# RWKV-7 scan: rows of beta and kappa swapped for the last four heads, right-hand sides laid out by chunk parity

## Chip, core and metric

The kernel runs on one core of a Trainium2 chip. The metric is device time in microseconds (us) of one execution; lower is better. Three timed runs of the kernel before are at hand, and one further execution was recorded by the hardware profiler.

Engine names as the profile has them: PE is the matrix engine and PEld its weight loads, DVE the vector engine, ACT the scalar engine, POOL the general one, SP the queue that issues nearly all DMAs. A name such as L592 is line 592 of the kernel before, unless the text says that it is a line of the changed kernel.

## What is computed

Two decoder layers on 512 tokens of width 1024. In each layer a gated FFN, then three token mixers beside each other on one normalised input (RWKV-7, latent attention, HGRN2), then a second FFN. The change lies in RWKV-7 alone, whose core is this recurrence over the tokens, for 8 heads of width 64:

```
def step(state, inp):
    r_t, w_t, k_t, v_t, kk_t, a_t = inp
    sa = jnp.einsum('bhvk,bhk->bhv', state, -kk_t)
    state = (state * w_t[:, :, None, :]
             + sa[..., None] * (kk_t * a_t)[:, :, None, :]
             + v_t[..., None] * k_t[:, :, None, :])
    return state, jnp.einsum('bhvk,bhk->bhv', state, r_t)
```

## The kernel before

**Chunks.** The recurrence is done in 8 chunks of 64 tokens (`CH`, `NC`). A head pair p (0 to 3) holds heads 2p and 2p+1; e picks the head in the pair; four tiles t of 128 tokens hold two chunks each, and u is the chunk's parity. Partitions 0 to 63 and 64 to 127 are the halves `U[0]` and `U[1]`.

**Before the scan.** `prep_keys` writes, for each pair, `BK`: beside each other in the columns of a tile beta and kappa (keys times the rate `a`, and keys), so that the matmul L483 of `rwkv_invert` puts beta products of a chunk of parity u in rows `U[u]` of the matrix `GM`, and kappa products in rows `U[1-u]`. L486 masks them on DVE. `prep_v` transposes the values; since kappa rows sit in the half that is not the chunk's own, ACT first copies the values with the two chunks of a tile exchanged (L453, two copies per pair). L489 (ACT) gathers the 32x32 diagonal blocks. L492 to L507, 31 steps of two DVE operations between transposes, invert them. L524 and L527 (PE, 32x32 tiles) join the blocks to `tt`, the inverse of each chunk.

**The scan** (`rwkv_scan`). First L567 forms the part of each right-hand side that comes from the values, and L568 copies it to `gv`. Then, for each chunk c of parity u:

- L575 (ACT) copies the values into the kappa half of `zv`;
- L583 (PE) multiplies the state by alpha, 8 matmuls, all into rows `U[u]`, one bank of PSUM for each e;
- L586 (DVE) adds `gv`: four additions on 64 partitions;
- L592 (PE) multiplies by the inverse: 8 matmuls, all reading and writing the half `U[u]`;
- L593 (ACT) negates the result into the other half of `zv`;
- L599 (PE) forms the new state's increment, L603/L605 and L607 (DVE) the new state;
- L611 and L615 (PE) form the output and L617 (ACT) stores it.

Each step needs the one above it. An fp32 matmul of this part is one row of the instruction order and two records of the trace (8 rows of L583, x16 in the trace).

**Fill.** So that PE has something to do meanwhile, projections of the other two mixers and of the gates are mixed in. One unit is 24 matmuls of 128x512 (L251 to L253), here called fills. `pump` releases units at named places by the table `PUMP`; a scheduler in the framework then decides at build time, by its own model of times, between which instructions of PE's queue the fills go, and the order on every other engine. The engines follow that order strictly. The weights of a unit are split into two parts, one by ACT (L208) and one by DVE (L209).

Of the kernel before, what the change touches and what calls it, by code (L numbers as in the profile page):

```python
# [14 lines left out]
AF = mybir.ActivationFunctionType  # L15
ALU = mybir.AluOpType
# [4 lines left out]
P = 128  # L21
# [3 lines left out]
NT = T // P  # L25
# [4 lines left out]
CH = 64  # L30
# [276 lines left out]
class Rwkv:  # L307
# [88 lines left out]
    def prep_keys(self, p, l):  # L396


        nc = self.nc
        S = self.S  # L400
        k, sw, a, kk = S["k"], S["sw"], S["a"], S["kk"]
        ch = lambda x: x.rearrange("p (c x) -> p c x", x=CH)
        tu = lambda x: x.rearrange("p (t u x) -> p t u x", u=2, x=CH)
        nc.vector.scalar_tensor_tensor(kk[:, p, :], k[:, p, :], S["k_k"](p), kk[:, p, :], op0=ALU.mult, op1=ALU.mult)
        al, d = S["AR"][p // 2][:, p % 2, 0], S["AR"][p // 2][:, p % 2, 1]
        bk = S["BK"][p // 2][:, p % 2]
        di = self.t2()
        nc.scalar.activation(d, sw[:, p, :], AF.Exp, scale=-DECAY)
        nc.scalar.activation(di, sw[:, p, :], AF.Exp, scale=DECAY)

        nc.vector.tensor_mul(ch(al)[:, :, 1:], ch(kk[:, p])[:, :, 1:], ch(d)[:, :, :CH - 1])
        nc.scalar.copy(ch(al)[:, :, 0:1], ch(kk[:, p])[:, :, 0:1])
        nc.vector.tensor_mul(kk[:, p], kk[:, p], a[:, p])
        nc.vector.tensor_mul(bk[:, :, 0::3, :], tu(kk[:, p]), tu(di))

        nc.scalar.activation(a[:, p, :], a[:, p, :], AF.Identity, scale=self.vec("rwkv_k_a", l, p), bias=self.oka[:, 4 * l + p:4 * l + p + 1])
        nc.vector.tensor_mul(k[:, p, :], k[:, p, :], a[:, p, :])
        nc.vector.tensor_mul(bk[:, :, 1:3, :], tu(k[:, p]), tu(di))
        nc.gpsimd.tensor_copy(self.DL[:, p], ch(d)[:, :, CH - 1])

    def prep_r(self, p, l):
# [7 lines left out]
    def prep_v(self, p, l):  # L429


        nc = self.nc
        S = self.S
        r, v, vres = S["r"], S["v"], S["vres"]
        if p == 0:
            S["vn"] = self.slot(10, (P, NT, T))
            if vres is not None:
                S["vup"] = self.t2()
                nc.sync.dma_start(out=S["vup"][32:64, :], in_=self.a["rwkv_vres_up"][0])
        if vres is not None:  # L440
            ps = self.psum("a")
            nc.tensor.matmul(ps, S["vup"][32:64, p * P:(p + 1) * P], vres[32:64, :], start=True, stop=True)
            sg, vf = self.t2(), self.t2()
            nc.sync.dma_start(out=vf, in_=self.v_first[:, p, :])
            nc.scalar.activation(sg, ps, AF.Sigmoid, bias=self.vec("rwkv_v0", 0, p))
            nc.vector.tensor_sub(vf, vf, v[:, p, :])
            nc.vector.tensor_mul(sg, sg, vf)
            nc.vector.tensor_add(v[:, p, :], v[:, p, :], sg)
        elif l == 0:
            nc.sync.dma_start(out=self.v_first[:, p, :], in_=v[:, p, :])  # L450
        vs = self.t2(shape=(P, NT, 2, CH))
        for u in range(2):
            nc.scalar.copy(vs[:, :, 1 - u, :], v[:, p].rearrange("p (t u x) -> p t u x", u=2, x=CH)[:, :, u, :])  # L453
        ps = self.psum("a", (P, NT, 2, CH))
        for t in range(NT):
            self.transpose(ps[:, t].rearrange("p e x -> p (e x)"), vs[:, t].rearrange("p u x -> p (u x)"))
        mean = self.tile([P, 2 * NT], "mean", bufs=2)
        nc.vector.tensor_reduce(mean, ps.rearrange("p t e x -> p (t e) x"), axis=AX.X, op=ALU.add)
        nc.vector.scalar_tensor_tensor(S["vn"][:, :, p * P:(p + 1) * P].rearrange("p t (e x) -> p t e x", x=CH),
                                       mean.rearrange("p (t e) -> p t e", e=2).unsqueeze(3).broadcast_to([P, NT, 2, CH]), -1.0 / CH,  # L460
                                       ps, op0=ALU.mult, op1=ALU.add)
        ps = self.sums(self.ones64, r[:, p, :])
        nc.vector.tensor_mul(v[:, p, :], v[:, p, :], ps)

    def rwkv_invert(self):


        nc = self.nc
        S = self.S
        GM = S["GM"] = [self.slot(i, (P, 2, NC, P)) for i in (0, 1, 6, 7)]  # L470
        ad = self.m4((P, 4, 2, NT, 32))
        mask = self.c("tri").unsqueeze(1).broadcast_to([P, 4, P])
        for p in range(4):
            self.pump("A4", p)

            for i in range(2):
                ps = [self.psum("a", (P, 4, P)) for _ in range(2)]
                for c in range(4):
                    cc = 4 * i + c
                    for e in range(2):  # L480
                        q = slice(64 * e, 64 * e + 64)
                        bk = S["BK"][p // 2][q, p % 2].rearrange("p t z x -> p (t z x)")
                        nc.tensor.matmul(ps[e][:, c, :], bk[:, P * cc:P * cc + P], S["AR"][p // 2][q, p % 2, :, cc * CH:(cc + 1) * CH],  # L483
                                         start=True, stop=True)
                for e in range(2):
                    nc.vector.tensor_mul(GM[p][:, e, 4 * i:4 * i + 4, :], ps[e], mask)  # L486
            for b in range(4):
                q = slice(32 * b, 32 * b + 32)
                nc.scalar.copy(ad[q, p], GM[p][q, :, b // 2::2, 32 * (b % 2):32 * (b % 2) + 32])  # L489
        nc.sync.dma_start(out=self.yd, in_=S["v"])  # L490
        ac = [self.m4((P, 32, 32)) for _ in range(2)]
        nc.vector.transpose(out=ac[0].rearrange("p s t -> p t s"), in_=ad.rearrange("p a e t x -> p x (a e t)"))  # L492
        a, tmp = ac
# [15 lines left out]
        for i in range(2):  # L509
# [8 lines left out]
            for half in range(2):  # L518
                for n in range(16):
                    h, t = 4 * i + n // 4, n % 4  # L520
                    for u in range(2):
                        up, dn = slice(64 * u, 64 * u + 32), slice(64 * u + 32, 64 * u + 64)
                        if half == 0:
                            nc.tensor.matmul(n21[dn, n, :], GM[h // 2][up, h % 2, 2 * t + u, 32:64], tu[up, 16 * i + n, :],  # L524
                                             start=True, stop=True, tile_position=(64 * u, 64 * u + 32))
                        else:
                            nc.tensor.matmul(n21[up, n, :], x[dn, n, :], tt[dn, n, dn], start=True, stop=True,  # L527
                                             tile_position=(64 * u + 32, 64 * u))
# [20 lines left out]
    def rwkv_scan(self, l):  # L549
# [6 lines left out]
        al = lambda p: S["AR"][p // 2][:, p % 2, 0]  # L556
        rho = lambda p: S["AR"][p // 2][:, p % 2, 1]
        bk = lambda p, c: S["BK"][p // 2][:, p % 2].rearrange("p t (u z) x -> p (t u) (z x)", u=2)[:, c]
        gv = [self.m4((P, 2, 2, NT, CH)) for _ in range(2)]
        for p in range(4):  # L560
            self.pump("A7", p)
            ps = self.psum("a", (P, 2, NT, CH))
            for e in range(2):
                h = 2 * p + e
                for t in range(NT):
                    for u in range(2):
                        nc.tensor.matmul(ps[U[u], e, t, :], GM[p][U[1 - u], e, 2 * t + u, 0:64], vn[U[1 - u], t, 64 * h:64 * h + 64], start=True, stop=True)  # L567
            nc.scalar.copy(gv[p // 2][:, p % 2], ps)  # L568
        for c in range(NC):
            self.pump("A8", c)  # L570
            t, u = c // 2, c % 2
            ck = slice(c * CH, (c + 1) * CH)

            zv = self.t2(shape=(P, 4, 2, CH))
            nc.scalar.copy(zv[U[1 - u]], vn[U[1 - u], t].rearrange("p (h e x) -> p h e x", e=2, x=CH))  # L575
            if c == 0:
                rhs = lambda p, e: gv[p // 2][U[0], p % 2, e, 0, :]
            else:
                r = self.t2(shape=(P, 4, 2, CH))
                ps = [self.psum("a", (P, 4, CH)) for _ in range(2)]  # L580
                for p in range(4):
                    for e in range(2):
                        nc.tensor.matmul(ps[e][U[u], p, :], al(p)[U[e], ck], st[U[e], 0, p, :], start=True, stop=True)  # L583
                for i in range(2):
                    for e in range(2):
                        nc.vector.tensor_add(r[U[u], 2 * i:2 * i + 2, e, :], ps[e][U[u], 2 * i:2 * i + 2, :], gv[i][U[u], :, e, t, :])  # L586
                rhs = lambda p, e: r[U[u], p, e, :]
            z = self.psum("z", (P, 4, 2, CH))
            for p in range(4):
                for e in range(2):  # L590
                    h = 2 * p + e
                    nc.tensor.matmul(z[U[u], p, e, :], S["tt"][h // 4][U[u], (h % 4) * 4 + t, U[u]], rhs(p, e), start=True, stop=True)  # L592
            nc.scalar.activation(zv[U[u]], z[U[u]], AF.Copy, scale=-1.0)  # L593
            y = self.psum("y", (P, 4, CH))
            if c < NC - 1:
                ns = self.psum("n", (P, 4, CH))
# [824 lines left out]
```

## Time and profile before

| | |
|---|---|
| three runs, median (lowest to highest) | 2718.49 us (2716.76 to 2718.83) |
| the profiled execution, its own time | 2718.67 us |
| its span, first to last instruction | 2716.9 us |
| mean granted PE clock | 0.995 |
| scan of the first layer, L567 to the last L615 | 597.40 to 653.6 us |
| scan of the second layer ends (last L617) | about 2005.8 us |

In a timeline row the first number is the start, the second the length, both in us; xN counts merged records, and what stands in square brackets is the idle time before them and what ended it. A matmul's length is longer than the distance to the next one, since matmuls are pipelined; so what PE pays is read from the distance between starts. In the table of stretches PEclk is the clock that was granted to PE as a share of the full one.

### The profile page before, as it was taken

How to read it: one execution, taken by the hardware profiler on the slowest of the kernel's cores; microseconds unless marked ns; L12 is line 12 of the kernel's file. 1: busy time of each engine (PE TensorE's matmuls, PEld its weight loads, DVE VectorE, ACT ScalarE, POOL GpSimd, SP SyncE). 2: the span in 40 equal slices, each digit the busy share in tenths (PEclk: the TensorE clock that was granted, in tenths of full speed). 3: DMA queues.
4: the chain of work that ended last, by engine and by line, in shares of the span. 5: the costliest groups of instructions: out<-in, count | busy, mean ns of one | idle time of the engine just before them, and what ended most of it. 6: DMA issues, size and time to landing. Idle time of an engine off the chain costs nothing. (4 is left out here: it accounts for less than half of the span.)

```text
span 2716.9 us, 42586 instructions
## 1 busy us (share of the span) xinstructions
PE 2668.8 (98%) x17669; PEld 2319.0 (85%) x17669; DVE 1771.6 (65%) x2507; ACT 1342.8 (49%) x2129; POOL 58.1 (2%) x121
## 2 busy tenths in 40 slices
PE   8999999999999999999999999999999999999999
PEld 7999888877787789998899998877777877899987
DVE  6776377743866767785468764477448676678843
ACT  4544346345657544444344443464455585444532
POOL 0000010000000010000000000000000000100000
PEclk9999999989999999999999999999999999999999
DMA  4333332334421542333313333233353315322332
GB/s 143 108 110 124 120 113 95 117 113 141 135 92 55 183 163 64 123 104 115 124 61 96 103 131 128 97 106 106 101 171 110 100 67 180 140 94 94 112 114 78
DMA packets 223519, 307.72 MB, mean 113 GB/s; under 512 B 11857, under 2 KB 181053, under 8 KB 221789
## 3 DMA queue, kind: packets, MB, share of 16 engines
q1 hardware_dynamic: 223324, 304.99, 34.1%
q8 instruction: 139, 2.28, 0.3%
q14 instruction: 56, 0.45, 0.1%
HBM read 269.84 MB, written 35.13 MB: 112 GB/s over the span
## 5 line engine op out<-in xcount | busy, mean ns | idle before, releaser
L251 PE MATMUL b<-xhi,wh 128*128 128x256 f32 (+1 forms) x2176 | 734.4, 337 | 0.0
L253 PE MATMUL b<-xhi,wl 128*128 128x256 f32 (+1 forms) x2176 | 733.7, 337 | 0.0
L252 PE MATMUL b<-xlo,wh 128*128 128x256 f32 (+1 forms) x2176 | 732.0, 336 | 0.0
L208 ACT CAST wh<-ws 128x1024 fp32r<-128x1024 f32 (+5 forms) x448 | 393.5, 889 | 654.4 <-PE b L252 285.6
L209 DVE TENSOR_TENSOR wl<-ws,wh 128x1024 fp32r<-128x1024 f32 (+5 forms) x448 | 453.4, 1022 | 271.0 <-ACT wh L208 263.0
L251 PEld LDWEIGHTS b<-xhi,wh 128*128 128x128 f32 x2176 | 414.7, 191 | 43.9 <-issue 3.7
L253 PEld LDWEIGHTS b<-xhi,wl 128*128 128x128 f32 x2176 | 414.7, 191 | 40.9 <-issue 1.6
L252 PEld LDWEIGHTS b<-xlo,wh 128*128 128x128 f32 x2176 | 414.8, 191 | 40.5 <-issue 1.7
L252 PE MATMUL b<-s,wh 128*128 128x256 f32 (+1 forms) x1120 | 344.7, 308 | 1.7 <-DVE s L209 1.7
L251 PE MATMUL b<-s,wh 128*128 128x256 f32 (+1 forms) x1120 | 344.2, 308 | 0.0
L253 PE MATMUL b<-s,wl 128*128 128x256 f32 (+1 forms) x1120 | 343.7, 307 | 0.0
L208 ACT CAST wh<-m 128x1024 fp32r<-128x1024 f32 x144 | 151.3, 1051 | 230.4 <-PE b L252 98.9
L251 PE MATMUL b<-wh,t 128*128 128x512 f32 x576 | 224.2, 389 | 0.0
L252 PE MATMUL b<-wl,t 128*128 128x512 f32 x576 | 224.1, 389 | 0.0
L253 PE MATMUL b<-wh,t 128*128 128x512 f32 x576 | 224.1, 389 | 0.0
L251 PEld LDWEIGHTS b<-s,wh 128*128 128x128 f32 x1120 | 213.9, 191 | 11.9 <-DVE s L1006 1.2
L252 PEld LDWEIGHTS b<-s,wh 128*128 128x128 f32 x1120 | 214.0, 191 | 11.8 <-DVE s L209 2.2
L253 PEld LDWEIGHTS b<-s,wl 128*128 128x128 f32 x1120 | 214.0, 191 | 10.3 <-DVE wl L209 0.5
L209 DVE TENSOR_TENSOR wl<-m,wh 128x1024 fp32r<-128x1024 f32 x144 | 174.0, 1224 | 32.5 <-ACT wh L208 32.5
L209 DVE TENSOR_TENSOR t<-s,t 128x512 fp32r<-128x512 f32 x80 | 55.0, 691 | 158.5 <-PE b L252 154.4
L251 PEld LDWEIGHTS b<-wh,t 128*128 128x128 f32 x576 | 108.1, 188 | 23.0 <-ACT t L1204 0.6
L253 PEld LDWEIGHTS b<-wh,t 128*128 128x128 f32 x576 | 108.1, 188 | 22.4
(324 smaller groups left out, 3965.4 us busy)
## 6 DMA issues: line engine op xcount, KB each, us to landing
ws<-in_w_in_dram SPq DMA_DIRECT2D x58, 1024.0 KB
ws<-in_ffn_w_up_dram SPq DMA_DIRECT2D x44, 1024.0 KB
ws<-in_ffn_w_down_dram SPq DMA_DIRECT2D x44, 1024.0 KB
ws<-in_ffn_w_gate_dram SPq DMA_DIRECT2D x43, 1024.0 KB
gd<-f SPq DMA_DIRECT2D x48, 256.0 KB
t<-gd SPq DMA_DIRECT2D x48, 256.0 KB
s<-cd SPq DMA_DIRECT2D x8, 1024.0 KB
ws<-in_w_o_dram SPq DMA_DIRECT2D x8, 1024.0 KB
```

What stands on the lines that cost most here:

```text
L208: self.nc.scalar.copy(hi, src)
L209: self.nc.vector.tensor_sub(lo, src, hi.bitcast(F32))
L251: nc.tensor.matmul(out, whi, xhi, start=start, stop=False, **kw)
L252: nc.tensor.matmul(out, whi, xlo, start=False, stop=False, **kw)
L253: nc.tensor.matmul(out, wlo, xhi, start=False, stop=stop, **kw)
```

## The change

For pairs 2 and 3 (the last four heads) beta and kappa change places in `BK`. Their rows in `GM` change halves with them: for these pairs the chunk's own products now lie in half `U[1-u]`. `prep_v` needs no exchanging copy for these pairs and transposes the values directly. `gv` is now indexed by parity (two buffers, one for each u) instead of by pair.

In the scan, `B = (U[u], U[1 - u])` gives the half of a pair: `B[0]` for pairs 0 and 1, `B[1]` for pairs 2 and 3. The right-hand sides of all eight heads so fill all 128 partitions, and two additions of 128x128 take the place of four of 64x128. The matmuls with alpha (L593 of the changed kernel) and with the inverse (L601 there) run in the order of pairs 0, 2, 1, 3, so that neighbours lie in different halves. The inverse's loop has e outside. The result is negated by two engines, ACT for `B[0]` (L602 there) and DVE for `B[1]` (L603 there), 64x256 each, and the values are copied into `zv` by two ACT copies of 64x256 (L585 there). The names of lines in the changed kernel: alpha L593, additions L595, inverse L601, increment L609, new state L613/L615, output L621 and L625.

```
-        nc.vector.tensor_mul(bk[:, :, 0::3, :], tu(kk[:, p]), tu(di))
+        sides = (bk[:, :, 0::3, :], bk[:, :, 1:3, :])
+        nc.vector.tensor_mul(sides[p // 2], tu(kk[:, p]), tu(di))
...
-        nc.vector.tensor_mul(bk[:, :, 1:3, :], tu(k[:, p]), tu(di))
+        nc.vector.tensor_mul(sides[1 - p // 2], tu(k[:, p]), tu(di))
...
-        vs = self.t2(shape=(P, NT, 2, CH))
-        for u in range(2):
-            nc.scalar.copy(vs[:, :, 1 - u, :], v[:, p].rearrange("p (t u x) -> p t u x", u=2, x=CH)[:, :, u, :])
+        vs = v[:, p]
+        if p < 2:
+            vs = self.t2()
+            for u in range(2):
+                nc.scalar.copy(vs.rearrange("p (t u x) -> p t u x", u=2, x=CH)[:, :, 1 - u, :], v[:, p].rearrange("p (t u x) -> p t u x", u=2, x=CH)[:, :, u, :])
...
-            nc.scalar.copy(zv[U[1 - u]], vn[U[1 - u], t].rearrange("p (h e x) -> p h e x", e=2, x=CH))
+            for i in range(2):
+                nc.scalar.copy(zv[B[1 - i], 2 * i:2 * i + 2], vn[B[1 - i], t].rearrange("p (h e x) -> p h e x", e=2, x=CH)[:, 2 * i:2 * i + 2])
...
-                r = self.t2(shape=(P, 4, 2, CH))
-                ps = [self.psum("a", (P, 4, CH)) for _ in range(2)]
-                for p in range(4):
+                r = self.t2(shape=(P, 2, 2, CH))
+                ps = [self.psum("a", (P, 2, CH)) for _ in range(2)]
+                for p in (0, 2, 1, 3):
                     for e in range(2):
-                        nc.tensor.matmul(ps[e][U[u], p, :], al(p)[U[e], ck], st[U[e], 0, p, :], start=True, stop=True)
-                for i in range(2):
-                    for e in range(2):
-                        nc.vector.tensor_add(r[U[u], 2 * i:2 * i + 2, e, :], ps[e][U[u], 2 * i:2 * i + 2, :], gv[i][U[u], :, e, t, :])
+                        nc.tensor.matmul(ps[e][B[p // 2], p % 2, :], al(p)[U[e], ck], st[U[e], 0, p, :], start=True, stop=True)
+                for e in range(2):
+                    nc.vector.tensor_add(r[:, e], ps[e], gv[u][:, :, e, t, :])
...
-            z = self.psum("z", (P, 4, 2, CH))
-            for p in range(4):
-                for e in range(2):
-                    h = 2 * p + e
-                    nc.tensor.matmul(z[U[u], p, e, :], S["tt"][h // 4][U[u], (h % 4) * 4 + t, U[u]], rhs(p, e), start=True, stop=True)
-            nc.scalar.activation(zv[U[u]], z[U[u]], AF.Copy, scale=-1.0)
+            z = self.psum("z", (P, 2, 2, CH))
+            for e in range(2):
+                for p in (0, 2, 1, 3):
+                    q = B[p // 2]
+                    nc.tensor.matmul(z[q, p % 2, e, :], S["tt"][p // 2][q, (2 * p + e) % 4 * 4 + t, q], rhs(p, e), start=True, stop=True)
+            nc.scalar.activation(zv[B[0], 0:2], z[B[0]], AF.Copy, scale=-1.0)
+            nc.vector.tensor_scalar(zv[B[1], 2:4], z[B[1]], -1.0, None, op0=ALU.mult)
```

The scheduler answers with another order. On PE, in a chunk of the first layer's scan, from the last fills after the alpha matmuls to the first increments, this stood there before (the third and the later L592 rows use the second `tt` buffer):

```order
L253 MATMUL b_801_5778<-xhi_92,wl_5775 128x512
L251 MATMUL b_801_5778<-xhi_92,wh_5774 128x512
L592 MATMUL b_787_5675<-t_5660,s_714_5075 64x64
L252 MATMUL b_801_5778<-xlo_93,wh_5774 128x512
L592 MATMUL b_787_5675<-t_5660,s_714_5075 64x64 x3
L592 MATMUL b_787_5675<-t_5660,s_715_5076 64x64 x4
L253 MATMUL b_801_5778<-xhi_92,wl_5775 128x512
L251 MATMUL b_801_5778<-xhi_92,wh_5774 128x512
L252 MATMUL b_801_5778<-xlo_93,wh_5774 128x512
L253 MATMUL b_801_5778<-xhi_92,wl_5775 128x512
L599 MATMUL b_789_5686<-t_5658,s_574_4140 64x64 x4
```

The same place on PE in the changed kernel, where L601 is the multiplication by the inverse:

```order
L253 MATMUL b_799_5774<-xhi_92,wl_5771 128x512
L601 MATMUL b_777_5612<-t_5599,s_712_5069 64x64
L601 MATMUL b_777_5612<-t_5599,s_713_5070 64x64
L601 MATMUL b_777_5612<-t_5599,s_712_5069 64x64
L601 MATMUL b_777_5612<-t_5599,s_713_5070 64x64
L601 MATMUL b_777_5612<-t_5599,s_712_5069 64x64
L601 MATMUL b_777_5612<-t_5599,s_713_5070 64x64
L601 MATMUL b_777_5612<-t_5599,s_712_5069 64x64
L601 MATMUL b_777_5612<-t_5599,s_713_5070 64x64
L251 MATMUL b_799_5774<-xhi_92,wh_5770 128x512
L252 MATMUL b_799_5774<-xlo_93,wh_5770 128x512
L253 MATMUL b_799_5774<-xhi_92,wl_5771 128x512
```

The eight inverse matmuls stand in one piece and alternate between the two buffers (and halves), where fills cut them in two or three pieces before. Counted from the first L567 to the last output matmul of one layer, the order of before has 88 fills in 29 pieces, that of after 83 fills in 20 pieces; the five others follow behind the scan. Both layers have the same counts.

In the second layer, on ACT, the end of the block gathering stood so before (L453 the exchanging copies of the last pair, L489 the gathering, `wh<-ws` a split of fill weights):

```order
L453 COPY t_17020<-s_2317_16176 128x4x64 x2
L208 CAST t_17032<-s_2315_16174 128x512
L489 COPY m_17043<-s_2464_17039 32x256 x4
L489 COPY m_17043<-s_2465_17040 32x256 x4
L489 COPY m_17043<-s_2466_17041 32x256 x4
L208 CAST wh_17297<-ws_17253 128x1024
L489 COPY m_17043<-s_2467_17042 32x256 x4
```

The same place in the changed kernel, where the gathering is L493:

```order
L208 CAST t_17022<-s_2313_16170 128x512
L493 COPY m_17033<-s_2460_17029 32x256 x4
L493 COPY m_17033<-s_2461_17030 32x256 x4
L493 COPY m_17033<-s_2462_17031 32x256 x4
L493 COPY m_17033<-s_2463_17032 32x256 x4
L208 CAST wh_17287<-ws_17243 128x1024
```

The copies are gone there, and the weight split stands behind the last gathering, no longer ahead of it. On PE the second layer has 9 fills fewer ahead of L524, which now come between L527 and the transposes of `BK` that follow it. On DVE one mask (L486) now stands ahead of the last pair's value statistics, and the weight split that stood ahead of L492 stands behind it. In the first layer the order ahead of the scan is the same on PE; there, and from some way behind the scan on, only single operations changed places.

More of the change, by code (lines that the diff above doesn't have):

```diff
@@ L450, in prep_v @@
             nc.sync.dma_start(out=self.v_first[:, p, :], in_=v[:, p, :])
-        vs = self.t2(shape=(P, NT, 2, CH))
-        for u in range(2):
-            nc.scalar.copy(vs[:, :, 1 - u, :], v[:, p].rearrange("p (t u x) -> p t u x", u=2, x=CH)[:, :, u, :])
+        vs = v[:, p]
[3 more added lines that the diff above has]
+                nc.scalar.copy(vs.rearrange("p (t u x) -> p t u x", u=2, x=CH)[:, :, 1 - u, :], v[:, p].rearrange("p (t u x) -> p t u x", u=2, x=CH)[:, :, u, :])
         ps = self.psum("a", (P, NT, 2, CH))
         for t in range(NT):
-            self.transpose(ps[:, t].rearrange("p e x -> p (e x)"), vs[:, t].rearrange("p u x -> p (u x)"))
+            self.transpose(ps[:, t].rearrange("p e x -> p (e x)"), vs[:, t * P:(t + 1) * P])
         mean = self.tile([P, 2 * NT], "mean", bufs=2)
@@ L488, in rwkv_invert @@
                 q = slice(32 * b, 32 * b + 32)
-                nc.scalar.copy(ad[q, p], GM[p][q, :, b // 2::2, 32 * (b % 2):32 * (b % 2) + 32])
+                nc.scalar.copy(ad[q, p], GM[p][q, :, (b // 2 + p // 2) % 2::2, 32 * (b % 2):32 * (b % 2) + 32])
         nc.sync.dma_start(out=self.yd, in_=S["v"])
@@ L523, in rwkv_invert @@
                         if half == 0:
-                            nc.tensor.matmul(n21[dn, n, :], GM[h // 2][up, h % 2, 2 * t + u, 32:64], tu[up, 16 * i + n, :],
+                            nc.tensor.matmul(n21[dn, n, :], GM[h // 2][up, h % 2, 2 * t + (u + i) % 2, 32:64], tu[up, 16 * i + n, :],
                                              start=True, stop=True, tile_position=(64 * u, 64 * u + 32))
@@ L559, in rwkv_scan @@
         gv = [self.m4((P, 2, 2, NT, CH)) for _ in range(2)]
-        for p in range(4):
-            self.pump("A7", p)
+        for n in range(4):
+            self.pump("A7", n)
+            u, k = n % 2, n // 2
             ps = self.psum("a", (P, 2, NT, CH))
             for e in range(2):
-                h = 2 * p + e
                 for t in range(NT):
-                    for u in range(2):
-                        nc.tensor.matmul(ps[U[u], e, t, :], GM[p][U[1 - u], e, 2 * t + u, 0:64], vn[U[1 - u], t, 64 * h:64 * h + 64], start=True, stop=True)
-            nc.scalar.copy(gv[p // 2][:, p % 2], ps)
+                    for s in range(2):
+                        p = k + 2 * ((u + s) % 2)
+                        h = 2 * p + e
+                        nc.tensor.matmul(ps[U[s], e, t, :], GM[p][U[1 - s], e, 2 * t + u, 0:64], vn[U[1 - s], t, 64 * h:64 * h + 64], start=True, stop=True)
+            nc.scalar.copy(gv[u][:, k], ps)
         for c in range(NC):
@@ L572, in rwkv_scan @@
             ck = slice(c * CH, (c + 1) * CH)
+            B = (U[u], U[1 - u])
             zv = self.t2(shape=(P, 4, 2, CH))
-            nc.scalar.copy(zv[U[1 - u]], vn[U[1 - u], t].rearrange("p (h e x) -> p h e x", e=2, x=CH))
+            for i in range(2):
+                nc.scalar.copy(zv[B[1 - i], 2 * i:2 * i + 2], vn[B[1 - i], t].rearrange("p (h e x) -> p h e x", e=2, x=CH)[:, 2 * i:2 * i + 2])
             if c == 0:
-                rhs = lambda p, e: gv[p // 2][U[0], p % 2, e, 0, :]
+                rhs = lambda p, e: gv[0][B[p // 2], p % 2, e, 0, :]
@@ L587, in rwkv_scan @@
-                rhs = lambda p, e: r[U[u], p, e, :]
-            z = self.psum("z", (P, 4, 2, CH))
-            for p in range(4):
-                for e in range(2):
-                    h = 2 * p + e
-                    nc.tensor.matmul(z[U[u], p, e, :], S["tt"][h // 4][U[u], (h % 4) * 4 + t, U[u]], rhs(p, e), start=True, stop=True)
-            nc.scalar.activation(zv[U[u]], z[U[u]], AF.Copy, scale=-1.0)
+                        nc.tensor.matmul(ps[e][B[p // 2], p % 2, :], al(p)[U[e], ck], st[U[e], 0, p, :], start=True, stop=True)
@@ new lines, in rwkv_scan @@
+                for e in range(2):
+                    nc.vector.tensor_add(r[:, e], ps[e], gv[u][:, :, e, t, :])
+                rhs = lambda p, e: r[B[p // 2], e, p % 2, :]
+            z = self.psum("z", (P, 2, 2, CH))
[4 more added lines that the diff above has]
+            nc.scalar.activation(zv[B[0], 0:2], z[B[0]], AF.Copy, scale=-1.0)
```

## Prediction

> **What bounds the kernel now.** First the page's head, for the busiest engine, then the table of stretches for the first layer's scan.
>
> ```profile
> span 2716.9 us, 42586 instructions
> PE 2668.8 (98%) x17669; PEld 2319.0 (85%) x17669; DVE 1771.6 (65%) x2507; ACT 1342.8 (49%) x2129; POOL 58.1 (2%) x121
> ```
>
> ```profile
> 597.00:660.00 63.00, 62.84 (x838) 47.24 (x836) 18.01 (x47) 26.48 (x52) 1.82 (x1) 1.00 0.37 121
> ```
>
> PE is busy for nearly the whole span and for 62.84 of 63 us here, at the full clock, while DVE and ACT are idle for over half. So a shorter step on DVE or ACT is worth what it takes out of PE's time. Third, the table of waits over 597 to 655 us:
>
> ```profile
> PEld b L592 <- issue: 2.9, 10, 0.4
> PEld b L592 <- DVE t L586: 2.8, 8, 0.4
> PEld b L599 <- ACT t L593: 2.5, 7, 0.4
> ```
>
> Ten times the inverse waits for nothing that the profile shows, and for as long (0.29 us on average) as it "waits" for the additions (0.35). These entries therefore look like the price of going from a fill to a scan matmul, not like waits for DVE. Fourth, the timeline, for that price:
>
> ```profile
> 597.40 2.08 PE L567 MATMUL b<-s,s 64*64 64x64 f32 x64
> ...
> 599.41 0.50 PE L251 MATMUL b<-xhi,wh 128*128 128x512 f32 x1
> ...
> 610.86 0.68 PE L583 MATMUL b<-t,s 64*64 64x64 f32 x16
> ...
> 611.47 0.50 PE L253 MATMUL b<-xhi,wl 128*128 128x512 f32 x1
> ...
> 613.05 0.68 PE L592 MATMUL b<-t,s 64*64 64x64 f32 x8
> ...
> 613.66 0.50 PE L251 MATMUL b<-xhi,wh 128*128 128x512 f32 x1
> ...
> 614.09 0.56 PE L592 MATMUL b<-t,s 64*64 64x64 f32 x6
> ...
> 614.58 0.50 PE L252 MATMUL b<-xlo,wh 128*128 128x512 f32 x1
> ...
> 614.91 0.39 PE L253 MATMUL b<-xhi,wl 128*128 128x512 f32 x1
> ...
> 615.14 0.39 PE L251 MATMUL b<-xhi,wh 128*128 128x512 f32 x1
> ...
> 615.68 0.69 PE L599 MATMUL b<-t,s 128*64 128x64 f32 x16
> ...
> 617.83 0.50 PE L253 MATMUL b<-xhi,wl 128*128 128x512 f32 x1
> ...
> 618.01 0.88 DVE L586 TENSOR_TENSOR t<-b,m 64x128 f32<-64x128 f32 x4 [0.71 <-PE b L583]
> ...
> 619.18 1.02 PE L592 MATMUL b<-t,s 64*64 64x64 f32 x14
> ...
> 620.14 0.50 PE L253 MATMUL b<-xhi,wl 128*128 128x512 f32 x1
> ...
> 652.97 0.68 PE L615 MATMUL b<-s,t 64*64 64x64 f32 x16
> ```
>
> Distances between starts give four prices. Fills follow each other every 0.23 us (614.91 to 615.14; I use 0.227). A piece of one fill takes 0.43 us (613.66 to 614.09), of four 1.10 (614.58 to 615.68): 0.227 each and 0.2 for the piece, say 0.21. The 16 records of L583 take 0.61 us, the 64 of L567 2.01 and the 64 from 615.68 to 617.83 (L599, L611, L615 and the next L583) 2.15: about 0.0305 a record and 0.12 for the piece. All of these alternate between halves of the array. L592 stays in one half: 8 records in 0.61 us, 6 in 0.49, 14 in 0.96, so 0.058 a record and 0.14 for the piece.
>
> As a test, one layer: 88 x 0.227 for fills, 29 x 0.21 for their pieces, 592 x 0.0305 and 128 x 0.058 for scan records, 30 x 0.12 for theirs: 55.2 us. Measured from 597.40 to 653.65: 56.2. About 1 us is left for all waits.
>
> **The change part by part.** *A, the inverse's order.* Its 8 matmuls per chunk alternate halves now. I price them like the alternating ones, at 0.0305: 16 records x 8 chunks x 2 layers = 256, times 0.0275 = 7.0 us less. If it brings nothing, 0.
>
> The Trainium skill, page "TensorEngine Tiling (Array Packing)", section "Gotcha 1: PSUM Pressure", says that different row tiles cannot access one bank of PSUM at the same time. The inverse writes one buffer `z` from both halves, so by it A would be 0, while L615, which also changes rows and writes one buffer `y`, is part of the piece at 0.0305, so the trace speaks against.
>
> *B, fewer pieces.* The order has 20 pieces of fills per layer for 29. Each costs 0.21 and the scan piece behind it 0.12. So 2 x 9 x 0.33 = 5.9 us less. The fills themselves are all still done (five per layer later): nothing.
>
> *C, additions, negation, copies.* Rows for their sizes:
>
> ```profile
> L586 DVE TENSOR_TENSOR t<-b,m x56: 272/288/297, 611.6 to 2000.5; 64x128 f32<-64x128 f32 x56
> ```
>
> ```profile
> L605 DVE TENSOR_TENSOR t<-b,t x12: 424/425/425, 616.4 to 1998.4; 128x256 f32<-128x256 f32 x12
> ```
>
> ```profile
> L593 ACT ACTIVATE t<-b x16: 592/592/598, 608.3 to 2003.1; 64x512 f32<-64x512 f32 x16
> ```
>
> ```profile
> L453 ACT COPY t<-s x16: 398/402/408, 476.5 to 1864.2; 128x256 f32<-128x256 f32 x16
> ```
>
> L586 at 128 columns takes 288 ns, L605 at 256 columns 425: two additions of 128x128 should take 0.29 each, against 0.88 for four. The first then is ready some 0.5 us after the alphas, and the order has two fills there (2 x 0.227 + 0.21 = 0.66). The negation of 64x256 should take ACT 0.4 (L453, as many columns; L593, twice as many, 0.59) and DVE at most 0.43 (L605), under three fills (0.89). So C is worth nothing beyond what B counts. Where it is uncovered: in two chunks per layer DVE's negation is queued behind a weight split L209 (1.22 us, a row below), and the increment on PE waits for it. It costs 0 if the split is done before, up to 1 us in each of four places; I take 0, since L209 in the order is released well ahead, and keep 4 for the range. The two `zv` copies cost ACT some 0.2 us per chunk more, in its idle half.
>
> *D, ahead of the second layer's join.* Fifth, the timeline of that place:
>
> ```profile
> 1868.05 0.68 DVE L486 TENSOR_TENSOR s<-b,consts 128x512 f32<-128x512 f32 x1
> ...
> 1882.11 1.05 ACT L208 CAST wh<-ws 128x1024 fp32r<-128x1024 f32 x1 [2.08 <-PE b L252]
> 1883.06 1.65 ACT L489 COPY m<-s 32x256 f32<-32x256 f32 x4
> 1883.19 1.22 DVE L209 TENSOR_TENSOR wl<-ws,wh 128x1024 fp32r<-128x1024 f32 x1 [1.37 <-ACT wh L208]
> ...
> 1914.57 0.39 PE L253 MATMUL b<-xhi,wl 128*128 128x512 f32 x1
> 1919.46 3.56 PE L524 MATMUL b<-m,s 32*32 32x32 f32 x128 [4.50 <-DVE m L507]
> ```
>
> PE ends its last fill at 1914.80 and stands until 1919.46, 4.66 us, for the inversion on DVE. That chain is now shorter. The gathering L489 started only when L208 had ended; its masks had ended at 1881.8 (in the order L208 now stands behind): about 1.15 us. Further ahead two copies of 0.40 (L453) fall away, one mask of 0.68 (the first L486) is done earlier, and 8 fills (1.8 us) no longer stand before the long run of L483. I take 1.8 + 0.7 = 2.5 for these, since PE and not the copies fed that run; if it is DVE after all, little. So the chain ends 3.7 us earlier (1.2 to 3.7). But 9 fills (2.0 us) moved behind the join, so PE arrives 2.0 earlier. Net gain 1.6 us (from a loss of 0.8), and PE stands for 4.66 + 2.0 - 3.7 = 3.0 us.
>
> *E, the clock behind that gap.* Sixth, the table of stretches round both joins (PEclk is the number ahead of the last two), and the rows of the work:
>
> ```profile
> 557.60:561.00 3.40, 0.00 (x0) 0.00 (x0) 3.40 (x2) 1.39 (x3) 0.00 (x0) 1.00 1.00 354
> 561.00:564.40 3.40, 2.98 (x113) 3.01 (x115) 2.59 (x5) 2.67 (x5) 0.00 (x0) 0.51 0.25 92
> ...
> 1916.20:1919.60 3.40, 0.14 (x9) 0.17 (x11) 3.40 (x3) 1.94 (x4) 0.00 (x0) 1.00 0.27 77
> 1919.60:1923.00 3.40, 3.40 (x129) 3.34 (x124) 2.03 (x4) 2.13 (x4) 0.00 (x0) 0.50 0.02 5
> 1926.40:1929.80 3.40, 3.40 (x10) 2.72 (x9) 0.69 (x1) 3.21 (x6) 0.00 (x0) 0.50 0.02 5
> 1929.80:1933.00 3.20, 3.20 (x78) 2.72 (x77) 0.90 (x2) 1.71 (x3) 0.00 (x0) 1.00 0.21 82
> ```
>
> ```profile
> 574.46 1.30 PE L527 MATMUL b<-s,t 32*32 32x32 f32 x64
> ...
> 1924.53 1.92 PE L527 MATMUL b<-s,t 32*32 32x32 f32 x64
> ```
>
> In both layers a stretch of 3.4 us with PE (nearly) idle is followed by half the clock; in the second for three stretches, to 1929.8. The 11 fills in them pay 0.425 for 0.227 (1926.40:1929.80 holds 10 rows in 3.40 us, with one switch), 2.2 us; L527 pays 1.92 for 1.30, 0.62; L524, with 128 records, I put at twice that, 1.24. Together 4.0 us. A gap of 3.0 us holds no empty stretch of 3.4, so I forecast that the drop goes in the second layer. In the first the order ahead is unchanged, and with it the gap and the drop.
>
> The Trainium skill, page "TensorE: Matmul & The Clock Gate", section "Part 1: The HAM clock gate (the "warmup" mystery)", describes a gate that throttles or releases the array's clock by how busy it has lately been; both drops above agree with it, and how short a gap still escapes no row here shows.
>
> *The sum.* 7.0 + 5.9 + 0 + 1.6 + 4.0 = 18.5 us. The profiled execution took 2718.67 us (1.8 outside its span), 0.2 above the median of 2718.49; 2718.5 - 18.5 = 2700. Behind the scan only single operations moved; I allow 1.5 us either way.
>
> **The rivals.** *The drop stays* in the second layer, if D brings 0.4 us less than I put it at and the gap stays over 3.4: 2700 + 4 = 2704. For it: 1916.20:1919.60 was not quite empty either. *Alternation brings nothing*, as each matmul waits until the half before it is out of the bank: A falls away, 2700 + 7 = 2707; against it the price of the piece with L615. *The first layer's drop goes too*: its gap is 4.2 us, near the border; another 4 to 5 us, 2695.5. *The chain of a chunk becomes the bound*: with 5 fills fewer and fewer pieces between alpha and increment, additions and negation come too late and PE waits before each inverse and increment. This decides at 18.5/14 = 1.32 us in each of the 14 chunks with a predecessor: there the time is that of before, and at 1.9 us each it is 2726. For it: DVE's negation behind L209; against it: in the waits of before no single one is over 0.4 us, and each wait would need a loss of about 0.7 beyond its cover.
>
> **How the numbers follow.** Forecast 0.55, drop stays 0.20, no gain of alternation 0.08, both drops gone 0.07, the chain bounds but only eats the gain 0.06, the chain makes it slower 0.04. The range goes from 2693 (both drops gone and 2.5 off) to 2708 (no alternation, or the drop and 4 us at the splits), which holds the first four. Within 0.2% (5.4 us, about what a measurement of this kernel can tell from no change) means over 2713: the fifth, 0.06; slower by more 0.04; the rest, 0.90, faster.
>
> **What would show it.** In the changed kernel's timeline: L601 in one piece of 16 records with about 0.6 us to the next fill (0.49 + 0.12), not 1.0; one scan 6.5 us shorter for the same fills; no wait over 0.5 us before L601 or L609; ahead of L528 a gap of about 3 us, and PEclk 1.00 behind it, with 0.50 behind the first layer's. The prediction is wrong if L601 keeps 0.058 a record, if waits for DVE or ACT of over 1 us stand in most chunks, or if the second gap is over 3.4 us.

## The result, and the profile after

The changed kernel takes 2702.0 us (median of 5 runs, 2700.41 to 2704.61), the kernel before 2718.49 beside it. The medians lie 16.5 us apart; the ratio on record is 0.9943 with a 95% interval of 0.9931 to 0.9954, which is 15.5 us less (12.5 to 18.8). Forecast were 18.5. The profiled execution is the longest of the five (2704.61 us); what makes it so is told below.

First the head of the page of the changed kernel, to be set beside that of before.

```profile
span 2702.6 us, 42584 instructions
PE 2654.7 (98%) x17669; PEld 2309.1 (85%) x17669; DVE 1771.4 (66%) x2495; ACT 1339.2 (50%) x2137; POOL 58.1 (2%) x121
```

PE's busy time fell by 14.1 us, all but 0.2 of what the span lost, and DVE and ACT are as busy as before: the gain lies on PE, in how its matmuls follow each other. The first layer's scan in the timeline of the changed kernel (L574 begins it, L593 alpha, L601 inverse, L625 ends it):

```profile
597.10 2.08 PE L574 MATMUL b<-s,s 64*64 64x64 f32 x64
...
609.68 0.46 PE L593 MATMUL b<-t,s 64*64 64x64 f32 x16
610.07 0.50 PE L252 MATMUL b<-xlo,wh 128*128 128x512 f32 x1
...
610.73 0.68 PE L601 MATMUL b<-t,s 64*64 64x64 f32 x16
611.35 0.50 PE L251 MATMUL b<-xhi,wh 128*128 128x512 f32 x1
...
643.34 0.68 PE L625 MATMUL b<-s,t 64*64 64x64 f32 x16
```

The inverse stands in one piece and takes 0.62 us to the next fill, as forecast; before, its pieces of 2, 8 and 6 or of 2 and 14 took 1.2 to 1.4 in all. Alpha takes 0.39, where L583 took 0.61; that was not forecast. The scan lasts from 597.10 to the next fill at 643.95, 46.85 us for 56.18, of which five fills (1.13) only moved behind it: 8.2 us saved.

Where the 14.3 us between the two spans come from is read from four instructions that both traces hold, one ahead of the first scan, one behind it, one ahead of the second scan and one behind it. Before:

```profile
503.58 0.39 PE L216 MATMUL b<-t,ones 128*128 128x512 f32 x1
...
735.53 0.45 PE L780 MATMUL b<-s 128*32 128x32 f32 x16 [0.50 <-DVE s L746]
...
1793.15 0.39 PE L215 MATMUL b<-t,ones 128*128 128x512 f32 x1
...
2087.96 0.45 PE L780 MATMUL b<-s 128*32 128x32 f32 x16 [0.55 <-DVE s L782]
```

The same four after the change:

```profile
503.32 0.39 PE L216 MATMUL b<-t,ones 128*128 128x512 f32 x1
...
727.09 0.45 PE L790 MATMUL b<-s 128*32 128x32 f32 x16 [0.50 <-DVE s L756]
...
1787.31 0.39 PE L215 MATMUL b<-t,ones 128*128 128x512 f32 x1
...
2073.77 0.45 PE L790 MATMUL b<-s 128*32 128x32 f32 x16 [0.55 <-DVE s L792]
```

The lead is 0.26, 8.44, 5.84 and 14.19 us. So the first layer gives 8.2, the second 8.35, and between them, where nothing was edited, 2.6 are lost. The second layer gives no more than the first, so the place ahead of its join (D) and the clock behind it (E) brought about nothing, where 5.6 had been forecast. Its timeline and stretches in the changed kernel (L490 mask, L496 the transpose that starts the inversion, L528 the join):

```profile
1873.99 1.29 DVE L490 TENSOR_TENSOR s<-b,consts 128x512 f32<-128x512 f32 x2 [0.44 <-PE b L487]
...
1876.99 2.26 DVE L496 STREAM_TRANSPOSE m<-m 128x1024 f32<-128x1024 f32 x1 [1.72 <-ACT m L493]
...
1907.11 0.39 PE L253 MATMUL b<-xhi,wl 128*128 128x512 f32 x1
1911.62 3.18 PE L528 MATMUL b<-m,s 32*32 32x32 f32 x128 [4.12 <-DVE m L511]
...
1916.31 1.92 PE L531 MATMUL b<-s,t 32*32 32x32 f32 x64
```

```profile
1906.80:1910.20 3.40, 0.70 (x4) 0.23 (x2) 3.26 (x6) 0.43 (x1) 0.00 (x0) 1.00 0.59 218
1910.20:1913.60 3.40, 1.98 (x92) 2.01 (x93) 3.40 (x4) 2.50 (x5) 0.00 (x0) 0.81 0.00 0
1913.60:1917.00 3.40, 3.40 (x74) 2.59 (x70) 1.30 (x3) 3.15 (x6) 0.00 (x0) 0.50 0.02 5
```

The gap runs from about 1907.3 to 1911.62, 4.3 us by the distance of starts and not 3.0, and the clock falls to 0.50 soon after the join has begun. The same two DVE steps before:

```profile
1880.53 1.29 DVE L486 TENSOR_TENSOR s<-b,consts 128x512 f32<-128x512 f32 x2 [0.44 <-PE b L483]
...
1884.74 2.24 DVE L492 STREAM_TRANSPOSE m<-m 128x1024 f32<-128x1024 f32 x1 [0.33 <-ACT m L489]
```

With the lead of 5.84 taken off, the last masks come 0.7 us earlier and the transpose 1.9. The gathering gained the 1.2 us expected of it; the rest of the chain gained 0.7 and not 2.5. The 1.9 are as much as the fills that moved behind the join cost (9 x 0.227 = 2.0).

### The profile page after: what moved, and what is told of

It reads as the page before. It is cut to its first block, busy times and chain, and to the rows that moved or that the text cites. A ratio compares the mean times of both kernels' runs of the same rounds, so it can differ in the third digit from the quotient of the medians.

```text
span 2702.6 us, 42584 instructions
## 1 busy us (share of the span) xinstructions
PE 2654.7 (98%) x17669; PEld 2309.1 (85%) x17669; DVE 1771.4 (66%) x2495; ACT 1339.2 (50%) x2137; POOL 58.1 (2%) x121
## 5 line engine op out<-in xcount | busy, mean ns | idle before, releaser
L209 DVE TENSOR_TENSOR wl<-ws,wh 128x1024 fp32r<-128x1024 f32 (+5 forms) x448 | 453.4, 1021 | 277.2 <-ACT wh L208 265.7
L209 DVE TENSOR_TENSOR wl<-m,wh 128x1024 fp32r<-128x1024 f32 x144 | 174.0, 1223 | 33.8 <-ACT wh L208 33.8
L209 DVE TENSOR_TENSOR t<-s,t 128x512 fp32r<-128x512 f32 x80 | 54.8, 691 | 157.2 <-PE b L252 154.2
```

What stands on the lines that cost most here:

```text
L209: self.nc.vector.tensor_sub(lo, src, hi.bitcast(F32))
```

## The experiments

Each ran at least five times. The unaltered changed kernel is the first of them, and its 2702.63 us is the measure for the others. Its own five lie between 2700.85 and 2704.17, so a difference of about 1 us can't be told from none by the times; clearly slower are the four runs whose times all lie above these (the inverse one half after the other, four additions, one unit of fill more, eight unused matmuls). The kernel before, run beside each group, had medians of 2717.98 to 2718.50 us.

**The same kernel again.** No edit.

> The changed kernel once more, unaltered. Its first profile loses 2.6 us against the kernel before between 890 and 1750 us, far from any edit: 3.4 us at half clock at 1360, and a wait for a weight transfer of 1.2 us at 1747. Theory: these two are chance of one execution, so at least one of them is missing in this profile, and the median is 2702 within 2. Rival: the change causes them (it shifts everything behind it against the clock's windows and the transfers), so both are there again at the same places.

2702.63 us (2700.85 to 2704.17); the profiled execution took 2700.85 us. Its stretches round 1360 and 1740, and then those of the first profile:

```profile
1357.72:1361.13 3.41, 1.56 (x14) 1.36 (x14) 2.15 (x4) 1.64 (x5) 0.86 (x2) 1.00 0.00 0
1361.13:1364.54 3.41, 3.41 (x31) 3.41 (x31) 0.79 (x2) 0.37 (x1) 0.00 (x0) 1.00 0.00 0
...
1740.00:1750.00 10.00, 9.88 (x42) 7.30 (x41) 2.43 (x3) 3.87 (x6) 0.00 (x0) 1.00 0.31 97
```

```profile
1359.40:1362.80 3.40, 1.54 (x14) 1.35 (x12) 2.88 (x5) 1.39 (x3) 0.49 (x1) 0.99 0.00 0
1362.80:1366.20 3.40, 3.40 (x18) 3.40 (x17) 0.06 (x1) 0.00 (x0) 0.00 (x0) 0.50 0.00 0
1366.20:1369.60 3.40, 3.40 (x31) 3.40 (x30) 0.00 (x0) 0.23 (x1) 0.00 (x0) 1.00 0.00 0
...
1740.00:1750.00 10.00, 8.74 (x36) 6.37 (x35) 4.44 (x5) 3.96 (x5) 0.00 (x0) 1.00 0.02 9
```

Neither the half clock at 1360 nor the long wait at 1747 is there again, so the 2.6 us are chance of one execution and no part of the change. The gap itself, 1.85 to 2.11 us, is in all twelve profiles of this study, the one of before among them; behind it 3.4 us at half clock are found in six of them. In every profile the changes of the clock lie a whole number of 3.413 us apart (in the first profile of the changed kernel at 560.63, 574.29, 1362.77 and 1366.18, among others). Laid on that grid, the gap lies whole in one stretch in all six profiles that have the drop. In five of the others two stretches share it, with at most 1.76 us in either. In the last, the one shown first above, it lies whole in one stretch (PE busy 1.56 of 3.41 us) and the clock stays all the same. So the place of the gap accounts for eleven of the twelve, and 1.85 us idle of 3.41 looks near the border.

**The inverse in pairs of one half.**

```
-                for p in (0, 2, 1, 3):
+                for p in range(4):
                     q = B[p // 2]
```

> The inverse in the order of pairs 0, 1, 2, 3 within each e: halves 0 0 1 1 0 0 1 1, 4 of 7 neighbours in one half where none was; the order on every engine else the same. Theory (a neighbour in the same half costs, 7 of them made the 7.0 us of term A): 4/7 of 7.0, 4 us slower than the changed kernel, and the 16 records take about 0.85 us to the next fill for 0.62. Rival (only the cutting by fills made L592 dear): no difference, 0.62.

2703.73 us, 1.1 slower. In its timeline the inverse takes 0.66 us for 0.62:

```profile
610.39 0.73 PE L601 MATMUL b<-t,s 64*64 64x64 f32 x16
611.05 0.50 PE L251 MATMUL b<-xhi,wh 128*128 128x512 f32 x1
```

The theory falls: 0.05 us in each of 14 chunks is 0.7 us, far below 4, and a neighbour in the same half costs little by itself. The rival's time nearly holds, but its reason does not: before, 14 records of one half that no fill cut still took 0.96 us (619.18 to 620.14).

**Alpha in the order of pairs.**

```
-                for p in (0, 2, 1, 3):
+                for p in range(4):
                     for e in range(2):
                         nc.tensor.matmul(ps[e][B[p // 2], p % 2, :], al(p)[U[e], ck], st[U[e], 0, p, :], ...
```

> The products with alpha in the order of pairs 0, 1, 2, 3: the half that is read still changes at each matmul, the half that is written only once in 8; the order else the same. Theory: in the changed kernel the 16 records take 0.39 us to the next fill, before they took 0.61, and this comes from the half that is written; so 0.61 again and 14 x 0.21 = 3 us slower. Rival (the shorter time comes from something else, such as smaller PSUM tiles): 0.39 still, no difference.

2703.32 us, 0.7 slower. The 16 records take 0.41 us:

```profile
622.77 0.47 PE L593 MATMUL b<-t,s 64*64 64x64 f32 x16
623.18 0.50 PE L251 MATMUL b<-xhi,wh 128*128 128x512 f32 x1
```

My theory on the order falls here too. Still the alphas of before, which read both halves and wrote one, took 0.61, and these, which write both, take 0.39 to 0.41 in either order. Set beside each other: L592, one half read and the same half written, 0.058 a record; L583, both read, one written, and L601, two halves in turn, 0.0305; L593, both read and both written, (0.39 - 0.12) / 16 = 0.017. The pace goes with the number of quarters of the array that a piece uses (one, two, four), and 0 0 1 1 does nearly as well as 0 1 0 1. A quarter is here one half read together with one half written. That it is the quarters, and not something else that alpha's new tiles brought, no run shows by itself. This run speaks in part against it: in its order each run of four matmuls uses two quarters only, as L583 did, and yet 0.2 of the 0.22 us stay won, where the inverse in runs of three and four (the next experiment) loses half.

**The inverse one half after the other.**

```
-            for e in range(2):
-                for p in (0, 2, 1, 3):
+            for p in range(4):
+                for e in range(2):
```

> The inverse pair by pair, 0 1 2 3, with e inside: all of one half first, then all of the other; the scheduler puts one fill behind the first matmul in most chunks. Theory (what counts is that a piece holds work for both halves, not which neighbours it has; pairs 0 0 1 1 cost only 0.05 us a chunk): 7 such chunks per layer pay one more piece each, 14 x 0.33 = 4.6 us, and the rest of the piece stays near 0.0305 a record; 2707. Rival (runs in one half pay 0.058 a record): 16 x 12 x 0.0275 = 5 us more on top, 2712.

2712.03 us, 9.4 slower: the rival's number, but in the timeline of one chunk the pace lies between the two:

```profile
610.82 0.33 PE L601 MATMUL b<-t,s 64*64 64x64 f32 x2
611.07 0.50 PE L251 MATMUL b<-xhi,wh 128*128 128x512 f32 x1
611.50 0.85 PE L601 MATMUL b<-t,s 64*64 64x64 f32 x14
612.28 0.50 PE L252 MATMUL b<-xlo,wh 128*128 128x512 f32 x1
```

The 14 records, three matmuls of one half and then four of the other, take 0.78 us; in one half alone they took 0.96 before, and 14 that alternate take 0.61 (in the run with four additions). So with runs of three and four about half of what alternation brings is lost. A chunk pays 0.25 + 0.78 - 0.62 = 0.41 and 0.21 for the piece of fills, and 14 x 0.62 = 8.7 of the 9.4 us are found. Of the 0.62, 0.17 is the missing alternation and the rest, 0.45, the cut: 2.4 us for the rival's 5, and 6.3 for the 4.6 that both gave the cut, so it is luck that the rival's sum came out.

**Four additions.**

```
+                for s in range(2):
                     for e in range(2):
-                    nc.vector.tensor_add(r[:, e], ps[e], gv[u][:, :, e, t, :])
+                        nc.vector.tensor_add(r[U[s], e], ps[e][U[s]], gv[u][U[s], :, e, t, :])
```

> The changed kernel with four additions of 64x128 per chunk (each e, each half) for the two of 128x128. The order then has 24 pieces of fills per layer for 20, and 5 fills more within the scan. Theory (only the pieces cost, term B): 2 x 4 x 0.33 = 2.6 us slower than the changed kernel, about 2705. Rival (the additions themselves lie on the path): two more of 0.29 us in each of 14 chunks, 8 us slower, 2711.

2706.65 us, 4.0 slower. In three chunks of the layer the order cuts the inverse again (L602 here), 0.26 + 0.61 and two more fills:

```profile
615.56 0.33 PE L602 MATMUL b<-t,s 64*64 64x64 f32 x2
615.82 0.50 PE L252 MATMUL b<-xlo,wh 128*128 128x512 f32 x1
...
616.47 0.68 PE L602 MATMUL b<-t,s 64*64 64x64 f32 x14
617.08 0.50 PE L251 MATMUL b<-xhi,wh 128*128 128x512 f32 x1
```

Three cuts at 0.26 + 0.21 and one more piece at 0.33 make 1.7 us a layer, 3.5 in two: the theory's kind, at a higher price (a cut piece of the inverse costs 0.47, not 0.33). The rival's 8 us did not come. The additions act through the order that they let the scheduler choose.

**ACT negates both halves.**

```
-            nc.vector.tensor_scalar(zv[B[1], 2:4], z[B[1]], -1.0, None, op0=ALU.mult)
+            nc.scalar.activation(zv[B[1], 2:4], z[B[1]], AF.Copy, scale=-1.0)
```

> ACT negates both halves, 64x256 each, one after the other, and DVE none; the order of PE stays nearly as it was (82 fills in 19 pieces per layer). Theory (negations lie under three fills, 0.89 us, term C): the second half comes 0.35 to 0.4 us later and is still covered, so within 1 us of the changed kernel's 2702.6. Rival (the split of the negation over two engines is worth its length): 14 x 0.4 = 5.6 us slower, 2708.

2702.9 us, no difference, so the negation on DVE buys nothing. But the run does not test what the theory says, that a later second half is still covered. In the changed kernel the two negations never ran beside each other; DVE's starts when ACT's has ended, here and in all 16 chunks:

```profile
611.46 0.38 ACT L602 ACTIVATE t<-b 64x256 f32<-64x256 f32 x1 [1.67 <-PE b L601]
611.88 0.42 DVE L603 TENSOR_SCALAR t<-b 64x256 f32<-64x256 f32 x1 [1.19 <-ACT t L602]
```

There the second half is ready 1.57 us after the inverse began (610.73 to 612.30), with ACT alone after 1.51 (610.51 to 612.02): it comes no later at all. Why DVE waits for ACT was not tried. With ACT alone the scan of a layer is 46.01 us long for 46.85, with one fill fewer in it, so about 0.6 shorter; in the whole time that does not show.

**The copies of before, for all pairs.**

```
-        vs = v[:, p]
-        if p < 2:
-            vs = self.t2()
-            for u in range(2):
-                nc.scalar.copy(vs...[:, :, 1 - u, :], v...[:, :, u, :])
+        vs = self.t2()
+        for u in range(2):
+            nc.scalar.copy(vs...[:, :, 1 - u if p < 2 else u, :], v...[:, :, u, :])
```

> The changed kernel, but ACT copies the values of pairs 2 and 3 too before they are transposed (straight, not exchanged). With this the order ahead of the second layer's join is that of the kernel before again (150 fills in the last piece, masks and weight split where they stood). Theory: parts D and E brought nothing, since the inversion's chain came 2.0 us earlier but 2.0 us of fills moved behind the join, and the clock halves there in any case: within 1 us of 2702.6. Rival: they brought what was forecast, 1.6 (D) or 5.6 us (D and E): 2704.2 or 2708.2.

2703.61 us, 1.0 slower, at the edge of what can be told: it rules out the 5.6 us of D and E, but not D's 1.6 alone. The profiles rule that out too: from the L215 of the four instructions above (1785.18 here) to the first matmul of the second scan (1940.69) it takes 155.51 us, in the two profiles of the changed kernel 156.01 and 155.59, and 155.95 before. D and E together bring nothing that shows.

**One unit of fill more ahead of the join.**

```
-    ... "A9": tuple(int(j in (2, 7, 12, 17, 22)) for j in range(31)), ...
+    ... "A9": tuple(int(j in (2, 7, 12, 17, 22, 27)) for j in range(31)), ...
```

> One unit of fill more is released late in the inversion, at step 27, so 22 fills more (5.0 us) stand ahead of the join in the second layer, and about as many in the first; they are missing at the end of the mixers. Theory (the gap ahead of the join is pure idle time of PE, and the half clock behind it is due to the gap): both gaps, 4.2 and 4.3 us, and both stretches of half clock, about 4 us each, go, 16 us faster than the changed kernel, 2686. Rival 1 (the clock drops for another reason, such as the 32x32 matmuls, which use little of the array): only the gaps, 2693. Rival 2 (the splits of the unit's weights lengthen the inversion on DVE, and the units are missed later): 2700 or more.

2706.55 us, 3.9 slower: rival 2 by its time, but not by its reason. The first layer's join in the timeline, and the stretches from 561.0:

```profile
561.82 2.21 PE L528 MATMUL b<-m,s 32*32 32x32 f32 x128
...
569.01 3.64 PE L531 MATMUL b<-s,t 32*32 32x32 f32 x128 [3.61 <-ACT t L536]
```

```profile
561.00:564.40 3.40, 3.40 (x134) 2.88 (x134) 0.41 (x1) 3.33 (x6) 0.00 (x0) 1.00 0.23 82
564.40:567.80 3.40, 1.00 (x5) 0.47 (x3) 1.52 (x2) 3.34 (x6) 0.00 (x0) 0.94 0.00 0
```

The gap ahead of the join is gone and the join runs at full clock, 2.21 us. Then PE waits 3.6 us for ACT, which copies the blocks and the join's first half (3.3 of 3.4 us busy), and the clock falls behind this gap instead. The gap ahead of the join was ACT's time to catch up too. The inversion on DVE did not get longer: from its first transpose to the first of those that end it are 30.70 us in the second layer, as in the run with no edit. In that layer a gap of 2.27 us is left, and the clock falls behind it as well:

```profile
1911.16 2.91 PE L528 MATMUL b<-m,s 32*32 32x32 f32 x128 [2.27 <-DVE m L511]
```

The rest of the 3.9 us was not taken apart.

**Unused matmuls in the gap.** Eight in the second layer alone, or four in each layer; they are computed and read by nothing.

```
+        hot = self.psum("y")
+        for _ in range(4):
+            nc.tensor.matmul(hot, self.c("ident"), a.rearrange("p s t -> p (s t)")[:, :512], start=True, stop=True)
         for j in range(31):
             self.pump("A9", j)
```

> The changed kernel with four matmuls more per layer that no result uses (fp32, 128x512, about 0.85 us each), ahead of the inversion's steps. They push the fills behind them 3.4 us into the gap ahead of the join, which should shrink from 4.2 to about 1.3 us in both layers. Theory (the half clock follows a window of 3.4 us of which PE idles about half or more; the gap is the cause): both stretches of half clock go, 4 us in each layer, 2694. Rival 1 (the join's 32x32 matmuls hold the clock down whatever stands ahead): the stretches stay, 2702.6. Rival 2 (the matmuls cost their length, as the gap is not slack): 2709.

2703.19 us, no clear difference (2699.87 to 2707.19): rival 1 by its time, but not by its reason. In the first layer the gap is gone and the join runs at full clock in 2.21 us; then PE waits 1.70 us for ACT, and 6.8 us at half clock follow. In the second layer 3.05 us of gap are left, not 1.3, with half the clock behind:

```profile
1907.82 3.17 PE L531 MATMUL b<-m,s 32*32 32x32 f32 x128 [3.05 <-DVE m L514]
```

> As the run with four unused matmuls, but eight (6.8 us), in the second layer alone; 15 fills (3.4 us) move behind the join, so the gap ahead of the second layer's join should shrink from 4.3 to about 0.9 us; the first layer is as in the changed kernel. Theory (a gap that leaves a window of 3.4 us less than half idle leaves the clock alone): the clock stays 1.00 through the join, L524's successor takes about 2.2 us for 3.6, and the 6.8 us of extra work are paid by 3.4 us of gap and about 4 us of clock: 2702 within 1.5. Rival 1 (the join itself brings the clock down): 0.50 behind it as ever, 2706. Rival 2 (a faster PE only waits for ACT behind the join, as it did for 1.7 us in the first layer of the run with four): full clock through the join, then a gap, and 2704 to 2706.

2708.35 us, 5.7 slower. The second layer of the run with eight:

```profile
1911.47 2.21 PE L532 MATMUL b<-m,s 32*32 32x32 f32 x128
...
1917.92 3.05 PE L535 MATMUL b<-s,t 32*32 32x32 f32 x128 [2.87 <-ACT t L540]
```

```profile
1914.40:1917.80 3.40, 0.65 (x3) 0.19 (x1) 2.61 (x3) 3.34 (x6) 0.00 (x0) 1.00 0.07 9
1917.80:1921.20 3.40, 3.28 (x130) 3.25 (x131) 2.88 (x6) 2.52 (x5) 0.00 (x0) 0.65 0.98 296
```

This is rival 2 of the last expectation in kind, though 2708.35 is above its 2704 to 2706: no gap, a join at full clock in 2.21 us, then 2.9 us of waiting for ACT and half the clock behind that. Rival 1 falls: the join's small matmuls alone don't bring the clock down.

## Why the prediction was right, and where it was not

- **What bounds the kernel** was read rightly: PE's issue, not its waits. The waits table of the changed kernel's scan still has its two entries, at the same 0.4 us at most, while the steps that they name changed their lengths (two additions for four, a negation of half the width):

```profile
PEld b L601 <- DVE t L595: 2.6, 7, 0.4
PEld b L609 <- ACT t L602: 2.6, 7, 0.4
```

- **A and B** were forecast at 12.9 us, 6.5 a layer, and measured 8.2 in each layer, 16.4. Summed over one layer's scan by distances between starts, the pieces of fills gave 1.8, as priced. The inverse gave 5.4 where A and the scan pieces of B make 4.6: 9.0 us became 4.3 in seven chunks, and 0.7 fell away in the first, whose inverse is mixed with L567. The term that was put at nothing is alpha, which I had not looked at as a changed step: its matmuls now write both halves too, 0.22 us in each of seven chunks, 1.5. Against it stand 0.35 us for increments and outputs (32 records take 1.13 for 1.08 us) and 0.2 for two scan pieces more.
- **Alternation brings nothing** (the rival from one bank of PSUM) is refuted: L601 writes one tile `z` from both halves at 0.0305 a record. The Trainium skill, page "TensorEngine Tiling (Array Packing)", section "Gotcha 1: PSUM Pressure", keeps different row tiles out of one bank at a time without exception; here they write different partitions of it and the trace differs, so the measurement decides.
- **C** came out near nothing, as forecast, but not as pictured: the additions take 286 ns (L595), and the negations of 378 and 422 ns run one after the other, 0.84 us from the first's start to the second's end, just under the three fills of 0.89. The chunks with L209 ahead of DVE's negation cost nothing that shows, since L209 ends as ACT's half does (625.80 and 625.78 in one of them).

```profile
L595 DVE TENSOR_TENSOR t<-b,m x28: 279/286/292, 610.2 to 1986.5; 128x128 f32<-128x128 f32 x28
```

- **D failed in one row**: I let the chain gain 2.5 us, most of it because fewer fills stood ahead of the long run of L483. It gained 0.7: the last masks come only that much earlier, about one mask (0.68), which is done before. The run of masks starts where it did (1861.94 + 5.84 = 1867.78, before 1868.05), with 15 masks for 16, and in its last part pairs of masks follow each other every 1.73 us before and after, DVE waiting 0.44 for PE and PE 0.20 for DVE each time. The chain came 1.9 us earlier, what the moved fills took back: net about 0, not 1.6.
- **E failed with it**: the second gap, 4.3 us, is over the 3.4 that the prediction itself named as the sign that it is wrong there. Its rule was wrong as well. I took a gap under 3.4 us for safe. A gap of 1.86 us that fell within one stretch (PE busy 1.54 of 3.40 us at 1359.4) was followed by half the clock, and so were gaps of 2.27 and 3.05 us ahead of the second join in two experiments, so the 3.0 us would not have been safe. And where the gap was really closed, PE waited for ACT behind the join, and the clock fell there. *The drop stays*, the second likeliest case, is what happened. Its 2704, with the 3.5 us that A and B brought above my price and without D's 1.6, is 2704 - 3.5 + 1.6 = 2702.1, near the 2702.0 measured. The forecast was only 2 us off by luck: a gain that I had not seen made up for most of one that did not come.

No version tried beats the changed kernel; with both negations on ACT the time is the same.

## What to carry to other kernels

When small matmuls bound a stage, note which halves each uninterrupted piece reads and writes, for every group of matmuls that an edit touches, not only for the one it is about. A shorter step on an idle engine can pay through the order that a scheduler then chooses: price the pieces. Before you fill a gap, ask what else uses it: here ACT caught up in it, and what closed the gap opened another behind.

## What the runs showed of the hardware

- Pace of 64x64 fp32 matmuls per record, two records to a matmul: 0.058 us with one half read and the same written (L592), 0.0305 with two quarters in use (L583, L601), 0.017 with four (L593); that the number of quarters is the reason is not shown. In the inverse, orders 0 1 0 1 and 0 0 1 1 differ by 0.05 us in 16 records; 0 0 0 1 1 1 1 pays 0.17 in 14.
- The same gap of 1.85 to 2.11 us was followed by 3.4 us at half clock in six profiles and not in six others, in the changed kernel once each, so it differs from one execution to the next, and with it about 1.7 us of the time. The clock changes on a grid of 3.413 us; all six drops have the gap whole in one stretch of it, and five of the six profiles without have it shared by two. No run moved the gap on purpose.
- The join's 128 records of 32x32 take 2.21 us at full clock and 3.6 at half, and where the gap stands ahead of it the half clock lasts three or four stretches of 3.4 us, though PE is busy throughout in the second layer (10.24 of 10.24 us in the first profile of the changed kernel); behind the gap at 1360 it lasted one. What decides its length was not tried.
